# First stage of a hybrid encoder block: instructions in written order, five of eight row blocks of the conditioning matrix through TensorE, x loads behind the matrix

## The chip, the cores and the metric

The kernel runs on one core of one Trainium2 chip. The metric is the device time of one execution in microseconds (us). Before the change it is 1370.64 us, the median of 3 runs (1370.08 to 1372.82).

## The reference

One layer of a bidirectional encoder for 2048 tokens of width 1024, all in float32. What matters here is its beginning: a conditioning vector `c` makes three vectors of 1024 through a 1024 x 3072 matrix; two of them scale and shift the normalised tokens, which are then projected.

```python
mod = silu(c) @ w_ada + b_ada
shift, scale, gate = split(mod, 3)
h = rmsnorm(x, norm_w) * (1 + scale) + shift
proj = h @ w_in + b_in          # 9 groups of 512 columns and 16 gate columns
# neighbourhood attention on four groups, a two-way mLSTM on five and the gates
y = concat(na_out, ml_out) @ w_out
out = rmsnorm(x + gate * y, final_norm_w)
```

## The kernel before, in words

Tokens lie in four groups g of 512 (`GT`), each of four tiles `tt` of 128; the model width lies in eight blocks k of 128 (`KT`). h is kept transposed, width on the partitions, as a rounded part `hhi[g]` and the remainder `hlo[g]`; weights are split alike into `whi` and `wlo`. So each product is three matmuls (hi hi, hi lo, lo hi; L452 to L456 and L507). Weight blocks of 256 columns alternate between two slots: a (block 0 with the 16 gate columns, so 272) and b (block 1), then blocks 2, 3 and so on.

`start` (L209 to L400) is the first stage; `tok_blocks` (L582) follows and begins with block 2. In `start`:

- **x.** `load_x` (L222) loads a tile of x, 512 KB. `prep_x` (L228) squares it on ACT, takes reciprocal roots (`rsqrt`, 12 small steps: on POOL for the first group, else on DVE) and scales x (ACT for the first group, L239, else DVE, L241). x tiles of groups 0, 1 and 3 share four buffers, those of group 2 have a pool of their own.
- **The conditioning matrix.** Shift is part 0 and scale part 1, each in two quarters q of 512 columns. `ada_tile(part, q, kt)` (L243) loads one row block of a quarter, 128 x 512 (256 KB, seven buffers `wada`), and DVE multiplies it by its entry of silu(c) per partition and adds it to `acc`: eight row blocks a quarter, four quarters, 32 products (L249, L251). `columns` (L253) sums `acc` over the partitions with four 1-column matmuls against `ones` into the one PSUM buffer `sp`, which leaves the quarter as columns; ACT copies it and POOL adds the bias `bada`, and for the scale adds 1 and multiplies by `norm_w` (L260 to L266). The results are `shT` and `gT`.
- **h of group 0.** `turned(k)` (L270) transposes four x tiles on PE into PSUM `tp` (three buffers). `first_h(k)` (L275, k 0 to 3) makes hhi and h on ACT, hlo on POOL. For k 4 to 7 the scale is applied first (`scaled`, L283) and the shift later (`shifted`, L287), since the shift's second quarter comes last.
- **Projection.** `vo_first(g)` (L498) multiplies a whole group with slot a, k outermost, into four PSUM banks (`pp` has four): 12 matmuls per k. `vo_group` (L510) takes the sums out on DVE (L524, L526), and for slot b multiplies tile by tile, 24 matmuls each. The loop at L375 does this for every group. After each tile it steps a chain (`next_h`, L359) that prepares the next group's h (`make_h`, L293: transposes, hhi on ACT, h on DVE, hlo on POOL).
- **Stores and fills.** The output tile of a `vo_group` is stored by SP at the next flush; `table_fills` (L555) writes constants to nine tables in DRAM.

The program is written with a scheduler that orders the instructions of each engine by itself: before the change the order in `start` is the scheduler's, led by the order of the text. Nearly all loads are issued by SP, in order. An instruction that waits holds up those behind it on its engine or queue.

Of the kernel before, what the change touches and what calls it, by code (L numbers as in the profile page):

```python
# [8 lines left out]
F32 = mybir.dt.float32  # L9
F32R = mybir.dt.float32r  # L10
AF = mybir.ActivationFunctionType
ALU = mybir.AluOpType
# [3 lines left out]
P = 128  # L16
D = 1024
T = 2048
KT = D // P
NG = 4  # L20
GT = 512
# [8 lines left out]
BIG = 1e30  # L30
# [32 lines left out]
class Kernel:  # L63
# [64 lines left out]
    def small_loads(self):  # L128
        nc = self.nc
        nc.sync.dma_start(self.bcol, self.b_col)  # L130
        nc.sync.dma_start(self.cw, self.conv_w)
        nc.sync.dma_start(self.cb, self.conv_b)
        nc.sync.dma_start(self.mlw, self.ml_w)
        nc.vector.tensor_scalar(self.bcol[:, 0:4], self.bcol[:, 0:4], -0.125, None, ALU.mult)


    def phase1(self):
# [4 lines left out]
        self.hhi = [ht012.tile([P, KT, GT], F32R, name=f"hhi{g}") for g in range(3)]  # L142
        self.hlo = [ht012.tile([P, KT, GT], F32R, name=f"hlo{g}") for g in range(3)]
# [36 lines left out]

        self.phase1b(left, right)


    def stage_tile(self, name):
        self.stages.reverse()
# [23 lines left out]
    def start(self, left):  # L209
# [5 lines left out]
        nc.sync.dma_start(cact, self.cT)  # L215
        nc.scalar.activation(cact, cact, AF.Silu)
# [3 lines left out]
        xt = {}  # L220

        def load_x(tt):  # L222
            pool = early if tt // 4 == 2 else xp
            t = pool.tile([P, D], F32, tag="x", bufs=4, name=f"x_{tt}")
            nc.sync.dma_start(t, self.x[tt * P : (tt + 1) * P, :])
            xt[tt] = t

        def prep_x(tts):  # L228
            n = len(tts)
            ssq = xp.tile([P, n], F32, tag=f"ssq{n}", bufs=2, name=f"ssq_{tts[0]}")  # L230
            rst = xp.tile([P, n], F32, tag=f"rst{n}", bufs=2, name=f"rst_{tts[0]}")
            for i, tt in enumerate(tts):
                junk = xp.tile([P, D], mybir.dt.bfloat16, tag="junk", bufs=1, name=f"junk_{tt}")
                nc.scalar.activation(junk, xt[tt], AF.Square, accum_out=ssq[:, i : i + 1])
            nc.vector.tensor_scalar(ssq, ssq, 1.0 / D, EPS, ALU.mult, ALU.add)
            self.rsqrt(xp, rst, ssq, f"x{tts[0]}", nc.gpsimd if tts[0] == 0 else None)
            for i, tt in enumerate(tts):
                if tt < 4:
                    nc.scalar.activation(xt[tt], xt[tt], AF.Copy, scale=rst[:, i : i + 1])  # L239
                else:  # L240
                    nc.vector.tensor_scalar(xt[tt], xt[tt], rst[:, i : i + 1], None, ALU.mult)  # L241

        def ada_tile(part, q, kt):  # L243
            w = ada.tile([P, GT], F32, tag="wada", bufs=7, name=f"wada_{part}_{q}_{kt}")
            c0 = part * D + q * GT
            nc.sync.dma_start(w, self.w_ada[kt * P : (kt + 1) * P, c0 : c0 + GT])
            a = acc[:, c0 : c0 + GT]
            if kt == 0:
                nc.vector.tensor_scalar(a, w, cact[:, kt : kt + 1], None, ALU.mult)  # L249
            else:  # L250
                nc.vector.scalar_tensor_tensor(a, w, cact[:, kt : kt + 1], a, ALU.mult, ALU.add)  # L251

        def columns(part, q):  # L253
            ps = self.sp.tile([P, 4], F32, tag="sp", name=f"mod_{part}_{q}")
            j0 = part * 8 + 4 * q
            for j in range(4):
                nc.tensor.matmul(ps[:, j : j + 1], acc[:, (j0 + j) * P : (j0 + j + 1) * P], self.ones[:, 0:1], start=True, stop=True)
            dst = (self.shT, self.gT)[part][:, 4 * q : 4 * q + 4]
            if part or q == 0:
                nc.scalar.activation(dst, ps, AF.Copy)  # L260
                nc.gpsimd.tensor_tensor(dst, dst, bada[:, j0 : j0 + 4], ALU.add)
            else:
                nc.vector.tensor_add(dst, ps, bada[:, j0 : j0 + 4])
            if part:
                nc.gpsimd.tensor_scalar(dst, dst, 1.0, None, ALU.add)
                nc.gpsimd.tensor_tensor(dst, dst, nw[:, 4 * q : 4 * q + 4], ALU.mult)  # L266

        tps = {}

        def turned(k):  # L270
            tps[k] = self.tp.tile([P, GT], F32, tag="tp", name=f"tp_0_{k}")
# [30 lines left out]
            nc.vector.tensor_scalar(h, tp, self.gT[:, k : k + 1], self.shT[:, k : k + 1], ALU.mult, ALU.add)  # L302
            nc.gpsimd.tensor_tensor(lo, h, hi.bitcast(F32), ALU.subtract)

        for tt in range(4):
            load_x(tt)
        prep_x([0, 1, 2, 3])
        for kt in range(KT):
            ada_tile(1, 0, kt)
            if kt == 2:  # L310
                nc.sync.dma_start(bada, self.b_ada)
                nc.sync.dma_start(nw, self.norm_w)
        self.load_w(0, 0, (0,))
        rg = xp.tile([P, KT, 16], F32, name="rg")
        hi, lo = self.wslot[0]
        nc.sync.dma_start(rg, self.w_gate)
        nc.scalar.activation(hi[:, :, 256:], rg, AF.Copy)
        nc.gpsimd.tensor_tensor(lo[:, :, 256:], rg, hi[:, :, 256:].bitcast(F32), ALU.subtract)
        for kt in range(KT):
            ada_tile(0, 0, kt)  # L320
        columns(1, 0)
        for k in range(3):
            turned(k)
        columns(0, 0)
        for kt in range(KT):
            ada_tile(1, 1, kt)
        self.load_w(0, 0, (1,))
        self.chain = iter(())
        first = self.vo_first(0)
        for k in range(4):  # L330
            first_h(k)
            if k == 0:
                turned(3)
        for k in range(4):
            if k:
                turned(k + 3)
            if k == 2:
                columns(1, 1)
            next(first)
        for kt in range(KT):  # L340
            ada_tile(0, 1, kt)
            if kt >= 4:
                scaled(kt)
                if kt == 4:
                    turned(7)
        columns(0, 1)
# [7 lines left out]
        early_s = ExitStack()  # L354
        early = self.pool(early_s, "early", bufs=1)
        self.load_w(1, 1)
        self.small_loads()

        def next_h(tiles):  # L359
            for _ in range(2):  # L360
                yield
            prep_x(tiles)
            yield
            for k in range(0, KT, 2):
                make_h(tiles, k)
                make_h(tiles, k + 1)
                yield

        fills = self.table_fills()

        def fill(g):
            for _ in range(3 if g >= 2 else 0):
                next(fills, None)

        for g in range(NG):  # L375
            nxt = [4 * g + 4 + j for j in range(4)] if g < NG - 1 else []
            for tt in nxt:
                load_x(tt)
            if nxt:
                self.chain = next_h(nxt)  # L380
            if 0 < g < 3:
                for _ in self.vo_first(g):
                    pass
            self.vo_group(0, 0, g, g < 3)
            fill(g)
            if not nxt:
                self.load_w(2, 0)
                self.load_bias(2)
            self.vo_group(1, 1, g)
            fill(g)  # L390
            if g == 1:
                for _ in self.chain:
                    pass
                early_s.close()
                ht3 = self.pool(left, "ht3", bufs=1)
                self.hhi.append(ht3.tile([P, KT, GT], F32R, name="hhi3"))
                self.hlo.append(ht3.tile([P, KT, GT], F32R, name="hlo3"))
        for _ in fills:
            pass
        self.flush()  # L400
# [153 lines left out]

    def table_fills(self):  # L555
        nc = self.nc
        nc.gpsimd.memset(self.big, BIG)
# [1152 lines left out]
```

## Time and profile before

| | |
|---|---|
| median of 3 runs | 1370.64 us |
| profiled execution | 1360.06 us |
| its span | 1358.3 us |
| PE busy | 1284.1 us (95%), 8204 matmuls |
| DVE busy | 796.4 us (59%) |
| ACT busy | 517.8 us (38%) |
| POOL busy | 288.7 us (21%) |
| mean granted TensorE clock | 0.995 |
| DMA | 263.29 MB, mean 194 GB/s |

PE is TensorE's matmuls, PEld its weight loads, DVE VectorE, ACT ScalarE, POOL GpSimd, SP the engine that issues most DMAs. A row of a view in order of time reads: start, duration, engine, line of the kernel, operation, output<-inputs, shapes, count, and in brackets the idle time before it and what ended it. A matmul of two float32 operands is recorded as two instructions, so four 1-column matmuls of `columns` stand as x8; a transpose stands as one.

### The profile page before, as it was taken

The page shows a single profiled execution, that of the slowest core. Times are in us where ns is not written, and L with a number is a line of the kernel's source. Part 1 is how long each engine was busy: PE and PEld are TensorE (multiplying, and loading weights), DVE is VectorE, ACT ScalarE, POOL GpSimd, SP SyncE. Part 2 cuts the span into 40 slices and gives each one's busy share as a digit, 9 for nine tenths or more (in the row PEclk, how much of TensorE's full clock was granted, in tenths as well). Part 3 has the DMA queues.
Part 4 walks back from the last instruction along what each step waited for, and adds up shares of the span by engine and source line. Part 5 has one row for each costly group of instructions (what it writes and reads, how often), then busy time and mean ns, then how long its engine had stood idle before and what let it go on. Part 6 is the DMA issues. An engine that isn't in the chain of part 4 may idle for free.

```text
span 1358.3 us, 23412 instructions
## 1 busy us (share of the span) xinstructions
PE 1284.1 (95%) x8204; PEld 1099.9 (81%) x8204; DVE 796.4 (59%) x2436; ACT 517.8 (38%) x1113; POOL 288.7 (21%) x322
## 2 busy tenths in 40 slices
PE   2989899999899999999989999999999999999996
PEld 2989899999788787888878878778877777778785
DVE  6683623111274569156867868867737676666664
ACT  4642213344432323113313323313346565555552
POOL 4454301335301110001212102212202211212121
PEclk9999999999999999999999999999999999999998
DMA  9799533599877675564676777667688986768871
GB/s 330 219 287 238 190 101 103 138 227 229 217 161 193 137 188 158 174 172 140 202 203 190 235 233 204 215 182 203 177 265 244 217 216 179 185 176 194 201 184 47
DMA packets 244425, 263.29 MB, mean 194 GB/s; under 512 B 31943, under 2 KB 200135, under 8 KB 244307
## 3 DMA queue, kind: packets, MB, share of 16 engines
q1 hardware_dynamic: 161374, 190.38, 51.0%
q0 software_dynamic: 20496, 36.21, 11.1%
q10 hardware_dynamic: 62436, 35.20, 9.2%
q8 instruction: 65, 1.06, 0.3%
q14 instruction: 54, 0.43, 0.1%
HBM read 177.18 MB, written 92.72 MB: 199 GB/s over the span
## 4 chain that ended last, share of the span: by engine, by line
PE 39%; DMA 10%; DVE 7%; issue 6%; POOL 1%; SPq 1%; ACT 1%; ACTq 0%; POOLq 0%; DVEq 0%
PE pq L892 16%; PE y L1459 10%; DMA tab<-d_t 4%; DMA kv<-d_ck 3%; PE pT L1399 3%; PE pO L1414 2%; PE pS L1371 2%; DVE acc_q L834 2%; PE pi L1120 2%; PE px L1118 2%; PE dc L1066 1%; DMA hlo<-d_wo 1%; SPq L576 1%; PE a L1105 1%; DMA d_ck<-acc_k 1%
## 5 line engine op out<-in xcount | busy, mean ns | idle before, releaser
L892 PE MATMUL pq<-hhi,whi_a 128*128 128x512 f32 x512 | 207.7, 406 | 0.8 <-ACT u L797 0.8
L892 PE MATMUL pq<-hlo,whi_a 128*128 128x512 f32 x512 | 208.1, 406 | 0.0
L892 PE MATMUL pq<-hhi,wlo_a 128*128 128x512 f32 x512 | 207.3, 405 | 0.0
L892 PEld LDWEIGHTS pq<-hhi,whi_a 128*128 128x128 f32 x512 | 96.8, 189 | 18.0 <-ACT u L797 1.2
L892 PEld LDWEIGHTS pq<-hlo,whi_a 128*128 128x128 f32 x512 | 96.7, 189 | 16.6 <-issue 0.5
L892 PEld LDWEIGHTS pq<-hhi,wlo_a 128*128 128x128 f32 x512 | 96.8, 189 | 16.5
L1401 ACT ACTIVATE pt<-pT 96x384 f32<-96x384 f32 (+3 forms) x128 | 65.8, 514 | 84.5 <-PE pT L1399 81.6
L1380 ACT ACTIVATE pbuf<-pbuf,mn 128x480 f32<-128x480 f32 (+5 forms) x128 | 76.1, 596 | 52.3 <-DVE mn L1379 52.2
L1459 PE MATMUL y<-hhi,whi_a 128*128 128x512 f32 x256 | 90.6, 415 | 0.5 <-ACT whi_a L1429 0.5
L1459 PE MATMUL y<-hhi,wlo_a 128*128 128x512 f32 (+1 forms) x272 | 90.6, 399 | 0.2 <-ACT y L1466 0.2
L1379 DVE CUSTOM_DVE_ANT_0 pbuf<-pS,tab 128x480 f32<-128x480 f32 (+5 forms) x128 | 63.0, 539 | 38.4 <-PE pS L1371 29.3
L1142 POOL TENSOR_TENSOR hm<-hm,ck 128x128 f32<-128x128 f32 x64 | 26.3, 412 | 268.4 <-DVE hm L1141 228.2
L866 POOL TENSOR_TENSOR wlo_a<-rawq,whi_a 128x1024 fp32r<-128x1024 f32 x20 | 48.3, 2413 | 153.3 <-ACT whi_a L865 115.3
L1123 ACT ACTIVATE num<-px,gtile 128x129 f32<-128x129 f32 x120 | 38.3, 364 | 109.5 <-PE px L1118 92.3
L1050 DVE TENSOR_SCALAR wv<-kv,gtile 128x129 f32<-128x129 f32 x120 | 37.8, 323 | 65.7 <-DMA kv<-d_ck 33.1
L524 DVE TENSOR_TENSOR stvo<-pvo,brow 128x256 f32<-128x256 f32 x64 | 26.4, 420 | 82.0 <-PE pvo L456 63.4
L454 PE MATMUL pvo<-whi_b,hhi 128*128 128x256 f32 x256 | 74.2, 290 | 0.2 <-DVE gates L526 0.2
L1399 PE MATMUL pT<-ident,pbuf 128*128 128x128 f32 (+2 forms) x416 | 66.9, 274 | 7.7 <-DVE pbuf L1391 6.3
L1399 PEld LDWEIGHTS pT<-ident,pbuf 128*128 128x128 f32 (+2 forms) x416 | 50.4, 136 | 29.3 <-issue 8.9
L455 PE MATMUL pvo<-wlo_b,hhi 128*128 128x256 f32 x256 | 72.8, 284 | 0.0
L456 PE MATMUL pvo<-whi_b,hlo 128*128 128x256 f32 x256 | 72.8, 284 | 0.0
L739 ACT ACTIVATE dec<-dec,gtile 128x128 f32<-128x128 f32 x128 | 42.2, 392 | 57.2 <-POOL dec L732 44.3
(296 smaller groups left out, 3418.6 us busy)
## 6 DMA issues: line engine op xcount, KB each, us to landing
ck<-d_ck SPq DMA_DIRECT2D x64, 384.5 KB
kv<-d_ck SPq DMA_DIRECT2D x120, 128.5 KB
rawq<-in_w_main_dram SPq DMA_DIRECT2D x28, 512.0 KB
raw<-in_w_main_dram SPq DMA_DIRECT2D x20, 512.0 KB
d_ck<-stvo SPq DMA_DIRECT2D x16, 514.0 KB
x<-in_x_dram SPq DMA_DIRECT2D x16, 512.0 KB
wada<-in_w_ada_dram SPq DMA_DIRECT2D x32, 256.0 KB
dec<-d_mneg SPq DMA_DIRECT2D x32, 256.0 KB
```

The lines of the kernel that those rows point to most:

```text
L454: nc.tensor.matmul(ps, lhi(k), rhi(k), start=(k == 0), stop=False)
L455: nc.tensor.matmul(ps, lhi(k), rlo(k), start=False, stop=False)
L456: self.mark = nc.tensor.matmul(ps, llo(k), rhi(k), start=False, stop=(k == KT - 1))
L739: nc.scalar.activation(t[:, o, :], t[:, o, :], AF.Exp, bias=self.cols["g"][:, d, h, c : c + 1])
L866: nc.gpsimd.tensor_tensor(lo[:, :, cs], raw, hi[:, :, cs].bitcast(F32), ALU.subtract)
L892: self.mark = nc.tensor.matmul(patch_ps(ps) if patch else ps, w, self.htok(h, g, k, patch), start=(k == 0 and n == 0), stop=(k == KT - 1 a ...
L1123: nc.scalar.activation(num[:, d, :], px[:, d, :], AF.Copy, scale=self.cols["inter"][:, d, h, c : c + 1])
L1379: nc.vector.tensor_tensor_reduce(pt[:, :nk], ps, tabs[place[u]][j][:, :nk], 1.0, 3e38, ALU.add, ALU.min, mn)
L1380: nc.scalar.activation(pt[:, :nk], pt[:, :nk], AF.Exp, bias=mn, scale=-1.0, accum_out=sums[:, j : j + 1])
L1399: nc.tensor.transpose(ps[:cs, i, :], U[u][j][:, i * cs : (i + 1) * cs], self.ident)
L1401: nc.scalar.activation(t[:cs, :nch, :], ps[:cs, :nch, :], AF.Copy)
L1459: nc.tensor.matmul(y, m[:, k, :], w[k][:, cs], start=(k == 4 and n == 0), stop=(k == 3 and n == 2))
```

## The change

- `start` runs inside `manual_schedule`: each engine does its instructions in the order of the text, which is written out anew.
- Of the eight row blocks of a quarter, DVE still adds kt 0, 2 and 4 (`summed`). kt 1, 3, 5, 6 and 7 go to PE (`added`): the block itself is the stationary operand, in four pieces of 128 columns, and the column of silu(c) the moving one, so that the sums arrive in PSUM as columns at once. DVE's three blocks join as a sixth `added` against `ones` (`total`), and the bias first of all, by a product with the identity. A quarter holds the one `sp` buffer from that product until `columns` reads it.
- `columns` is one operation: DVE for the scale ((sum + 1) x norm_w), ACT for the shift.
- Roots are on DVE for every group. `bada` and `nw` are loaded from ACT's queue.
- The x tiles of groups 1 and 2 are loaded into the room of hhi of a later group, so they need no free x buffer. They and group 3's are issued behind the last row block of the matrix.
- Transposes of the next group spread: k 0 to 3 beside slot b, k 4 after it, k 5 to 7 between the steps of `vo_first`, which group 3 uses too. Squares stand beside k 4 to 7.
- The `big` memset moves to the front, a scaling of `bcol` (`scale_bias`) behind group 1, a part of block 1's split from POOL to DVE, and the fills are spread anew. Block 2's weights are loaded and split beside group 3's slot b.

The core of the diff:

```diff
-        self.start(left)
+        with self.tc.manual_schedule():
+            self.start(left)
...
+        def summed(part, q, kt, w):
+            c0 = part * D + q * GT
             a = acc[:, c0 : c0 + GT]
             if kt == 0:
                 nc.vector.tensor_scalar(a, w, cact[:, kt : kt + 1], None, ALU.mult)
             else:
                 nc.vector.scalar_tensor_tensor(a, w, cact[:, kt : kt + 1], a, ALU.mult, ALU.add)
+        def added(ps, left, right, last):
+            for j in range(4):
+                nc.tensor.matmul(ps[:, j : j + 1], left[:, j * P : (j + 1) * P], right, start=False, stop=last and j == 3)
+
+        def quarter(part, q):
+            ws, parts = {}, iter([False] * 5 + [True])
+            ps = mods[part, q] = self.sp.tile([P, 4], F32, tag="sp", name=f"mod_{part}_{q}")
+            j0 = part * 8 + 4 * q
+            nc.tensor.matmul(ps, self.ident, bada[:, j0 : j0 + 4], start=True, stop=False)
+            def load(kt):
+                ws[kt] = ada_tile(part, q, kt)
+            def step(kt):
+                if kt in (0, 2, 4):
+                    summed(part, q, kt, ws.pop(kt))
+                else:
+                    added(ps, ws.pop(kt), cact[:, kt : kt + 1], next(parts))
+            def total():
+                c0 = part * D + q * GT
+                added(ps, acc[:, c0 : c0 + GT], self.ones[:, 0:1], next(parts))
+            return load, step, total
...
+        for tt in four:
+            load_x(tt)
+        load, step, total = quarter(1, 0)
+        for kt in range(KT):
+            load(kt)
...
+        for tt in four:
+            square(tt, ssq)
+        step(0)
+        rst = roots(four, ssq)
+        for kt in range(1, KT):
+            step(kt)
+        total()
+        columns(1, 0)
+        part = self.raw_w(0, 0, (0,))[0]
...
+        load, step, total = quarter(0, 0)
+        for kt in range(KT):
+            load(kt)
+        for tt in four:
+            scale_x(tt, rst)
+        part()
...
         for kt in range(KT):
+            step(kt)
+            if kt == 4:
+                for k in range(3):
+                    turned(k)
+                total()
         columns(0, 0)
+        load, step, total = quarter(1, 1)
...
+        first_h(0)
+        step(0)
+        step(1)
+        first_h(1)
+        next(first)
+        turned(3)
+        step(2)
+        step(3)
+        first_h(2)
+        next(first)
+        turned(4)
+        step(4)
+        step(5)
+        first_h(3)
+        next(first)
+        turned(5)
+        total()
+        step(6)
+        step(7)
+        part()
+        next(first)
+        turned(6)
+        columns(1, 1)
+        load, step, total = quarter(0, 1)
         for kt in range(KT):
+            load(kt)
+        step(0)
+        parts = self.raw_w(1, 1)
...
+        for tt in range(4, 8):
+            load_x(tt)
+        for k in range(4, KT):
+            step(k - 3)
+            scaled(k)
+            if k == 4:
+                turned(7)
+        step(5)
+        total()
+        step(6)
+        step(7)
+        columns(0, 1)
         for k in range(4, KT):
             shifted(k)
             next(first)
+        parts[0]()
+        parts[1](nc.vector)
...
+            self.vo_group(0, 0, g, True)
+            if tiles:
+                rst = roots(tiles, ssq)
+                for tt in tiles:
+                    scale_x(tt, rst)
```

More of the change, by code (lines that the diff above doesn't have):

```diff
@@ L141, in phase1 @@
         ht012 = self.pool(left, "ht012", bufs=1)
-        self.hhi = [ht012.tile([P, KT, GT], F32R, name=f"hhi{g}") for g in range(3)]
-        self.hlo = [ht012.tile([P, KT, GT], F32R, name=f"hlo{g}") for g in range(3)]
+        self.hpools = {g: ht012 for g in range(3)}
+        self.hhi, self.hlo = [], []
+        for g in range(2):
+            self.token_tiles(g)
         self.gcols = self.pool(right, "gcols", bufs=1, side="right")
@@ L181, in phase1, with token_tiles @@
         self.phase1b(left, right)
+    def token_tiles(self, g):
+        for part, held in (("hi", self.hhi), ("lo", self.hlo)):
+            held.append(self.hpools[g].tile([P, KT, GT], F32R, tag=f"h{part}{g}", name=f"h{part}{g}"))
     def stage_tile(self, name):
@@ L251, in ada_tile @@
                 nc.vector.scalar_tensor_tensor(a, w, cact[:, kt : kt + 1], a, ALU.mult, ALU.add)
-        def columns(part, q):
[L254 to L261, printed above, removed]
-            else:
[L263 to L268, printed above, removed]
+        def added(ps, left, right, last):
[11 more added lines that the diff above has]
+                    summed(part, q, kt, ws.pop(kt))
+                else:
+                    added(ps, ws.pop(kt), cact[:, kt : kt + 1], next(parts))
[3 more added lines that the diff above has]
+            return load, step, total
+        def columns(part, q):
+            qs = slice(4 * q, 4 * q + 4)
+            ps = mods.pop((part, q))
+            if part:
+                nc.vector.scalar_tensor_tensor(self.gT[:, qs], ps, 1.0, nw[:, qs], ALU.add, ALU.mult)
+            else:
+                nc.scalar.activation(self.shT[:, qs], ps, AF.Copy)
+        tps, mods = {}, {}
         def turned(k):
@@ L367, in next_h, with next_w @@
                 yield
+        def next_w():
+            for part in self.raw_w(2, 0):
+                yield
+                part()
         fills = self.table_fills()
-        def fill(g):
-            for _ in range(3 if g >= 2 else 0):
-                next(fills, None)
[L375 to L397, printed above, removed]
+        self.chain = iter(())
```

126 lines of the change are left out of this document (69 added, 57 removed).

## The prediction

> **What bounds the kernel now.** I read the page first, then the busy time of each engine by stage, then PE's instructions in order of time, then what the first of them waited for.
>
> ```profile
> span 1358.3 us, 23412 instructions
> ```
> ```profile
> 0.00:34.00 34.00, 9.05 (x36) 7.28 (x37) 21.36 (x30) 14.90 (x23) 14.44 (x29) 1.00 0.93 330
> 34.00:68.00 34.00, 32.03 (x238) 31.14 (x239) 20.52 (x44) 22.27 (x36) 14.22 (x11) 0.95 0.70 219
> 238.00:272.00 34.00, 34.00 (x290) 34.00 (x289) 5.69 (x15) 12.23 (x29) 12.37 (x8) 1.00 0.56 141
> ```
>
> The second fence is the table by stage; its columns are PE, PEld, DVE, ACT and POOL busy, granted clock, DMA share and GB/s. From 238 to 272 PE is busy for all 34 us: the kernel runs at PE's pace once it has started, and PE is nearly idle only in the first 34 us (9.05). So I take a delay or gain of PE in the first stage as a delay or gain of the end, one for one. PE's marks in that stage:
>
> ```profile
> 19.03 4.02 PE L273 MATMUL tp<-ident,x 128*128 128x128 f32 x12 [19.03 <-ACT x L239]
> 22.84 1.71 PE L257 MATMUL mod<-ones,acc 128*128 128x1 f32 x8
> 24.81 1.86 PE L257 MATMUL mod<-ones,acc 128*128 128x1 f32 x8 [0.26 <-ACT gT L260]
> 31.77 0.59 PE L507 MATMUL pvo<-whi_a,hhi 128*128 128x272 f32 x1 [5.09 <-ACT hhi L280]
> 45.85 0.39 PE L507 MATMUL pvo<-whi_a,hhi 128*128 128x272 f32 x1 [1.59 <-ACT hhi L290]
> 53.73 0.28 PE L454 MATMUL pvo<-whi_b,hhi 128*128 128x256 f32 x1
> 156.06 0.36 PE L454 MATMUL pvo<-whi_a,hhi 128*128 128x256 f32 x1 [1.30 <-DVE stvo L524]
> ```
>
> The first projection matmul starts at 31.77, the first group's slot-0 work ends at 53.73, and block 2, the first of the next stage, begins at 156.06. I forecast these three marks. What holds the first one:
>
> ```profile
> 9.19 1.06 ACT L234 ACTIVATE junk<-x 128x1024 bf16<-128x1024 f32 x1
> 10.83 0.63 POOL L1230 TENSOR_TENSOR nwt_x<-rst 128x4 f32<-128x4 f32 x1 [9.25 <-DVE rst L1217]
> 17.37 0.42 POOL L1233 TENSOR_TENSOR rst<-rst,nwt_x 128x4 f32<-128x4 f32 x1
> 27.10 2.33 POOL L203 TENSOR_TENSOR wlo_a<-raw,whi_a 128x1024 fp32r<-128x1024 f32 x1
> 30.26 0.65 POOL L261 TENSOR_TENSOR shT<-shT,bada 128x4 f32<-128x4 f32 x1
> 32.47 6.36 POOL L281 TENSOR_TENSOR hlo<-h,hhi 128x512 fp32r<-128x512 f32 x4 [1.56 <-ACT h L280]
> 30.94 0.78 ACT L280 ACTIVATE hhi<-tp,shT,gT 128x512 fp32r<-128x512 f32 x1 [4.05 <-POOL shT L261]
> 9.89 0.49 DVE L249 TENSOR_SCALAR acc<-wada,cact 128x512 f32<-128x512 f32 x1 [8.87 <-DMA wada<-in_w_ada_dram]
> 10.65 5.47 DVE L251 SCALAR_TENSOR_TENSOR acc<-wada,cact,acc 128x512 f32<-128x512 f32 x7
> 32.88 8.86 DVE L251 SCALAR_TENSOR_TENSOR acc<-wada,cact,acc 128x512 f32<-128x512 f32 x7 [0.24 <-DMA wada<-in_w_ada_dram]
> ```
>
> The squares end at 10.3 (9.19 + 1.06). The reciprocal roots then take POOL 7 us (10.83 to 17.8). Two POOL jobs then stand before the shift's bias (27.10 to 30.26), and only then can ACT make the first h (30.94). DVE multiplies the matrix's row blocks at 5.47/7 = 0.78 us each, and the last quarter ends at 32.88 + 8.86 = 41.7, which PE feels as the 1.59 us at 45.85.
>
> **The change part by part.** *Roots to DVE.* The same roots of a later group show the price on DVE:
>
> ```profile
> 60.03 0.17 DVE L235 TENSOR_SCALAR ssq<-ssq 128x4 f32<-128x4 f32 x1
> 62.62 0.16 DVE L1233 TENSOR_TENSOR rst<-rst,nwt_x 128x4 f32<-128x4 f32 x1
> ```
>
> That is 2.8 us, so x is scaled from about 13.3 on, not 17.8. The gain is hidden if PE is late, and below it is. Biases folded into PSUM and into one DVE operation take POOL off the path (about 4 us). The two loads on ACT's queue (bada, nw) stand before the squares, in ACT's wait for x until 5.22 us; I cost them at nothing, and 0.9 us if that wait were gone.
>
> *Row blocks on PE.* A quarter now has six sums on PE (five blocks and a total), each of four 1-column products, and one identity product. Each sum is exactly one `mod` group of before, x8 in the rows. So 24 groups stand where 4 stood. Their price hangs on the clock:
>
> ```profile
> 38.51 0.95 PE L257 MATMUL mod<-ones,acc 128*128 128x1 f32 x8
> 39.32 0.38 PE L507 MATMUL pvo<-whi_a,hhi 128*128 128x272 f32 x1
> 32.16 0.43 PE L507 MATMUL pvo<-wlo_a,hhi 128*128 128x272 f32 x1
> 32.39 0.43 PE L507 MATMUL pvo<-whi_a,hhi 128*128 128x272 f32 x1
> 32.62 1.05 PE L273 MATMUL tp<-ident,x 128*128 128x128 f32 x4
> 103.69 0.29 PE L507 MATMUL pvo<-whi_a,hhi 128*128 128x272 f32 x1
> 115.63 0.29 PE L507 MATMUL pvo<-whi_a,hlo 128*128 128x272 f32 x1
> 116.55 0.36 PE L454 MATMUL pvo<-whi_b,hhi 128*128 128x256 f32 x1
> 119.48 1.04 PE L298 MATMUL tp<-ident,x 128*128 128x128 f32 x8
> 120.27 0.36 PE L454 MATMUL pvo<-whi_b,hhi 128*128 128x256 f32 x1
> ```
>
> Slow against fast: a sum takes 1.71 (22.84) or 39.32 - 38.51 = 0.81; twelve 272-column matmuls take 12 x 0.23 = 2.73 or 12 x (115.63 - 103.69)/95 = 1.51; four transposes take 1.05 or (120.27 - 119.48)/2 = 0.40. Which price holds? The granted clock in windows of 3.41 us:
>
> ```profile
> 22.59:26.01 3.42, 3.16 (x17) 3.07 (x15) 3.22 (x6) 1.32 (x3) 1.09 (x2) 1.00 0.97 337
> 43.07:46.49 3.42, 1.83 (x16) 1.66 (x14) 0.82 (x2) 3.42 (x7) 2.35 (x1) 1.00 0.00 0
> 46.49:49.90 3.41, 3.40 (x16) 3.26 (x15) 2.08 (x4) 2.08 (x3) 1.25 (x1) 0.50 0.68 180
> 780.35:783.77 3.42, 1.68 (x9) 0.99 (x7) 0.00 (x0) 1.38 (x4) 0.00 (x0) 1.00 1.03 334
> ```
>
> The clock column shows only what was granted again after a loss, so the slow start stands at 1.00. Two readings decide. In 22.59 to 26.01 PE is busy for 3.16 us, nearly all with 1-column products, and the products after it (24.81 + 1.86 = 26.67) are as slow as before. In 43.07 to 46.49 it is busy for 1.83 us, of which 0.95 are such products, and the clock falls to 0.50 in the next window; yet 1.68 us of 512-column matmuls at 780 cost nothing. I conclude that 1-column products do not count as work that earns the clock, and price sums slow wherever PE does little else.
>
> The Trainium skill, TensorE: Matmul & The Clock Gate, Part 1, speaks against this: about 3.4 us of sustained matmul activity release the full clock. By that rule PE, fed from 10.7 us on, would run its sums fast from about 16 on; that is rival B. Its Part 4 says that transposes do not count as PE-busy in the same way; no row here has transposes alone.
>
> *The schedule of PE, slow sums.* Row blocks land no faster than they do now, kt 1 by 10.65.
> - Quarter (1,0): 10.65 + 6 x 1.71 = 20.9. The next identity product waits for the one `sp` buffer until DVE has read it, 0.35 by the 0.26 wait at 24.81: 21.3.
> - Quarter (0,0): 0.43 + 6 x 1.71 + three transposes 3.15: 35.1. The shift is copied: 35.5.
> - ACT makes hhi 0 (0.78) and h (the same) by 37.0, POOL hlo 0 (6.36/4 = 1.59) by 38.5. PE does the identity and one sum of (1,1) meanwhile, so the first projection matmul starts at **37.6 against 31.77**; the third waits for hlo 0. k 0 ends at 40.8.
> - k 1 with a transpose and a sum: slow 5.49, fast 2.72. k 2 the same. k 3 with three sums and two transposes: slow 9.96, fast 4.74. Quarter (0,1) with one transpose: slow 11.74, fast 5.46. Columns and the shift of k 4: 1.2. k 4 to 7, 48 matmuls: 4.5 us slow, then fast, 8.0; all fast 6.0. (One window is 3.4 and two are 6.8; after the wait at 45.85 it was over at 49.90.)
> - My choice: k 1 slow (46.3), k 2 and k 3 fast since half of PE's time there is wide matmuls (53.8), one window of (0,1) fast and the last 2.6 sums slow (61.7), then 1.2 and 8.0: **70.9 against 53.73**. All slow is 82.7; all fast after k 0 is 63.6.
>
> DVE falls from eight products a quarter to three; what it gives up hides behind PE. What PE waits on is not the matrix's DMA: at the 330 GB/s of the first stage's row, the 2.1 MB of a quarter land in 6.4 us, against 10.3 of sums. The written order itself I cost at nothing outside this list: each engine's waits in it are the ones named here; what they may cost besides is bounded with the rest below, 0 to 9.7. Behind a sum that waits for its block stand the transposes and wide matmuls of the next k, which is why the list is added up in order.
>
> *Loads moved.* On SP the last block of (0,1) waits for DVE's first product of that quarter (about 54), and behind it stand block 1's weights, the biases and x 4 to 7. The splits on ACT and POOL and the squares on ACT wait for those: 3.1 MB at 330 GB/s are there by about 63.5, and ACT turns to the splits at 63 and to the squares at 65. That is hidden; with fast sums (rival B) the same loads would land at 50 for an ACT that is ready at 48, which costs up to 2 us. x 8 to 15 come a group early.
>
> *After 53.73.* Before takes 102.3 us to block 2. Its matmuls alone are three groups of 96 at 0.1257 (36.2), sixteen runs of 24 at 119.48 - 116.55 = 2.93 (46.9), and 24 transposed blocks at 0.40 (9.5): 92.6. The other 9.7 are waits and slow clock:
>
> ```profile
> PE tp L298 <- DVE h L302: 3.7, 3, 2.2
> 90.20 0.66 PE L298 MATMUL tp<-ident,x 128*128 128x128 f32 x4 [2.20 <-DVE h L302]
> 82.51 1.06 ACT L234 ACTIVATE junk<-x 128x1024 bf16<-128x1024 f32 x1 [7.88 <-DMA x<-in_x_dram]
> ```
>
> Late x (82.51) makes the late h that PE waits for at 90.20. With x there early, squares beside k 4 to 7 and transposes spread over k, I let 3 us remain, between 0 and 9.7 (nearer 0, since the largest has its cause removed; the 1.3 at 156 stays): 95.6, a gain of 6.7.
>
> *The sum.* 70.9 + 95.6 = 166.5 against 156.06: +10.4. On the profiled execution's 1360.06 (span 1358.3 and 1.8 around it) that is 1370.5; the median shown is 1370.64, 10.6 above that execution, so I add the difference to it: **1381.0**. The other cases use the same rest.
>
> **The rivals.**
> - B, the sums earn the clock. Three sums slow, then fast: (1,0) ends at 18.2, (0,0) with its copy at 25.2, k 0 at 29.5 (hlo 0 from POOL at 28.2), k 3 at 39.7, (0,1) at 45.1, slot 0 at 52.3. With the rest 147.9: -8.1, **1362.5, faster**. For it: nearly unbroken feeding from 10.7 on, six times longer than the sample at 22.59. Against: that window and the fall at 46.49. It decides from the point where 1-column products release the clock.
> - C, wide matmuls keep the clock through (0,1): 63.6, +3.1, **1373.8**. For it: 1.68 us of wide work were enough at 780. Against: (0,1) has none.
> - D, never fast before k 4: 82.7, +22.2, **1392.9**. For it: k 1 and 2 are only half wide matmuls, and less than that lost the clock at 43.07.
>
> **How the numbers follow.** A 0.50, B 0.24, C 0.13, D 0.13. A's own range, with 0 to 9.7 in the rest and the window's phase, is 1375 to 1388. The whole reaches to B and leaves out D: 1360 to 1389. Within 0.2% (2.7 us, about what a measurement tells apart) lies half of C: 0.07; faster 0.24, slower 0.69.
>
> **What would show it.** Right: the products at 11 to 35 us all near 1.7 per eight; DVE idle beside them; the first projection matmul near 37.6; PE free of waits for h after slot 0; block 2 near 166. Wrong: products falling to 0.8 per eight by 18 us (B), a clock of 1.00 through (0,1) (C), or a shift at block 2 that is not found at the end.

## The result and the profile after

| | before | after |
|---|---|---|
| median | 1368.18 us (18 runs, 1363.69 to 1372.82) | 1376.16 us (18 runs, 1371.45 to 1383.81) |
| ratio | | 1.0063, 95% interval 1.0047 to 1.0079 |
| profiled execution | 1360.06 us, span 1358.3 | 1382.7 us, span 1380.9 |
| second profile, see the experiments | 1367.42 us, span 1365.6 | 1369.45 us, span 1367.7 |

The kernel after is slower by 0.6%. The first profiled execution of before is below all its timed runs, and that of after near the top of its own; so 22.6 us between those two profiles overstate it, and a second profile of each stands beside them below. PE's marks, read in its order of time as in the prediction (us):

| | first projection matmul | slot 0 done | block 2 begins | conv stage begins | it ends | span |
|---|---|---|---|---|---|---|
| forecast | 37.6 | 70.9 | 166.5 | | | |
| after | 37.33 | 74.94 | 170.97 | 360.5 | 559.1 | 1380.9 |
| after, second profile | 36.77 | 68.48 | 162.15 | 350.1 | 543.8 | 1367.7 |
| before | 31.77 | 53.73 | 156.06 | 348.2 | 538.6 | 1358.3 |
| before, second profile | 31.40 | 53.99 | 153.14 | 347.1 | 540.1 | 1365.6 |

The conv stage, which follows the token stage that block 2 opens, is told from the others by its first `pc` and `pq` matmuls. The table of the kernel after by stage (PE, PEld, DVE, ACT and POOL busy, granted clock, DMA share, GB/s):

```profile
0.00:34.00 34.00, 23.30 (x109) 23.19 (x109) 7.67 (x25) 11.50 (x16) 3.69 (x9) 1.00 0.71 242
34.00:68.00 34.00, 32.72 (x176) 32.07 (x175) 3.78 (x7) 11.22 (x18) 7.44 (x5) 0.79 0.61 201
68.00:102.00 34.00, 34.00 (x271) 34.00 (x272) 19.93 (x47) 20.07 (x31) 12.73 (x13) 0.96 0.99 258
```

PE is busy for 23.30 us of the first 34 instead of 9.05, DVE for 3.78 us of the second 34 instead of 20.52. Work went from DVE, which had time, to PE, which sets the end. In the second stretch PE is busy as long as before (32.72 against 32.03), but with 176 matmuls in place of 238, at a clock of 0.79. PE in order of time:

```profile
11.01 8.67 PE L273 MATMUL mod<-cact,wada 128*128 128x1 f32 x40 [1.31 <-DMA wada<-in_w_ada_dram]
19.53 1.85 PE L273 MATMUL mod<-ones,acc 128*128 128x1 f32 x8
...
25.49 2.80 PE L309 MATMUL tp<-ident,x 128*128 128x128 f32 x12
28.09 1.71 PE L273 MATMUL mod<-ones,acc 128*128 128x1 f32 x8
29.65 5.26 PE L273 MATMUL mod<-cact,wada 128*128 128x1 f32 x24
...
37.33 0.57 PE L602 MATMUL pvo<-whi_a,hhi 128*128 128x272 f32 x1
...
41.29 1.71 PE L273 MATMUL mod<-cact,wada 128*128 128x1 f32 x8
...
46.57 0.99 PE L273 MATMUL mod<-cact,wada 128*128 128x1 f32 x8
...
62.49 3.55 PE L273 MATMUL mod<-cact,wada 128*128 128x1 f32 x16
67.06 0.59 PE L602 MATMUL pvo<-whi_a,hhi 128*128 128x272 f32 x1 [1.01 <-ACT hhi L326]
...
158.01 0.35 PE L549 MATMUL pvo<-whi_b,hhi 128*128 128x256 f32 x1 [2.05 <-DVE gates L621]
```

Read the counts: x40 is five sums of eight, in 8.67 us, 1.71 each and a small tail. From 11 to 20 PE does nothing but such products, without a gap, and they never get shorter; nor do they from 28 to 35. Between wide matmuls, at 46.57, one takes 0.99. Behind slot 0 PE waits only once more before block 2, 2.05 us at 158. Now the clock around the last sums, in windows of 3.41 us (in the kernel before, half clock lasts one such window, from 46.49 to 49.90; here it lasts 17.07 us, from 53.39 to 70.46, which is five windows):

```profile
49.98:53.39 3.41, 3.41 (x31) 3.41 (x30) 1.13 (x3) 0.97 (x2) 0.00 (x0) 1.00 0.27 72
53.39:56.80 3.41, 3.41 (x19) 3.41 (x18) 0.93 (x2) 0.98 (x2) 0.00 (x0) 0.51 0.76 233
...
67.04:70.46 3.42, 3.40 (x13) 3.12 (x14) 2.73 (x4) 3.42 (x5) 0.59 (x1) 0.50 0.05 20
70.46:73.87 3.41, 3.41 (x29) 3.41 (x28) 2.60 (x1) 3.35 (x6) 1.91 (x3) 0.99 0.81 256
```

PE is full in the window before the fall, 3.41 of 3.41 us, but its first 2.07 us are sums (to 52.05) and only 1.34 wide matmuls; the clock goes at 53.39. From 54.91 to 66.0 there are sums with four transposes between them; up to 63.63 PE is just as busy in each window, and the clock stays away. It is back at 70.46, behind the first full window of wide matmuls (from 67.06).

### The profile page after: what moved, and what is told of

Same layout as the page of the kernel before. It is cut to its first block, busy times and chain, and to the rows that moved or that the text cites. A ratio compares the mean times of both kernels' runs of the same rounds, so it can differ in the third digit from the quotient of the medians.

```text
span 1380.9 us, 23691 instructions
## 1 busy us (share of the span) xinstructions
PE 1325.0 (96%) x8372; PEld 1142.5 (83%) x8372; DVE 769.9 (56%) x2430; ACT 518.6 (38%) x1112; POOL 272.7 (20%) x302
## 4 chain that ended last, share of the span: by engine, by line
PE 41%; DMA 11%; issue 6%; DVE 5%; POOL 1%; ACT 1%; SPq 0%; ACTq 0%; DVEq 0%; POOLq 0%
PE pq L986 17%; PE y L1553 8%; DMA tab<-d_t 6%; DMA kv<-d_ck 3%; PE pT L1493 2%; PE pO L1508 2%; PE pc L551 2%; PE pc L550 2%; PE pc L549 2%; PE pi L1214 2%; PE pS L1465 2%; PE px L1212 2%; PE dc L1160 1%; DVE pbuf L1473 1%; DMA hlo<-d_wo 1%
## 5 line engine op out<-in xcount | busy, mean ns | idle before, releaser
L1474 ACT ACTIVATE pbuf<-pbuf,mn 128x480 f32<-128x480 f32 (+5 forms) x128 | 76.1, 595 | 53.8 <-DVE mn L1473 53.8
```

Source lines behind the costliest of these rows:

```text
L1474: nc.scalar.activation(pt[:, :nk], pt[:, :nk], AF.Exp, bias=mn, scale=-1.0, accum_out=sums[:, j : j + 1])
```

## The experiments

The first four ran on one chip, where before's median was 1363.37 us; the next four on another (1364.74), the last three on a third (1362.87). Ratios are to before on the same chip.

**All row blocks on VectorE.** Order, roots and early x loads stay as after; no row block goes through TensorE.

```diff
-            ws, parts = {}, iter([False] * 5 + [True])
+            ws, parts = {}, iter([True])
-                if kt in (0, 2, 4):
+                if True:
```

(`total` moves behind the last step of each quarter.)

> The changed kernel with all eight row blocks of every quarter on DVE again (PE only sums DVE's result, one group of eight 1-column products a quarter); the written order, the roots on DVE and the early x stay. If the sums on PE at half clock are the whole loss: DVE is done with quarter (1,0) at 18.7, PE's sum at 20.6, (0,0) at 26.7 and 28.5, the first projection matmul at 29.7 (37.33 in the changed kernel, 31.77 before); slot 0 of the first group ends near 55 (74.94 and 53.73), block 2 begins near 149.5 (156.06 before), so about 0.995 of the time before. Rival, the written order is the loss and the products only stand in it: the first projection matmul stays near 37, slot 0 near 75, and the time stays at 1.006.

1355.4 us, ratio 0.9941 (0.9919 to 0.9963): faster than both. First matmul at 30.41, slot 0 done at 58.62, block 2 at 151.96. The direction is as expected, slot 0 and block 2 are 2 to 4 us late. The profile says why:

```profile
27.46 1.87 PE L273 MATMUL mod<-ones,acc 128*128 128x1 f32 x8 [2.78 <-DVE acc L269]
...
47.72 1.87 PE L273 MATMUL mod<-ones,acc 128*128 128x1 f32 x8 [3.48 <-DVE acc L269]
```

Now PE waits for DVE's products, 2.78 and 3.48 us. So DVE did need relief in this order, but the price paid for it was higher. What remains of the change without the sums is a gain of 0.6%. Only the sums were undone here, so it is they that turn this gain into a loss.

**Wide matmuls between the sums.** To the kernel after: thirty 512-column bf16 matmuls of no use ahead of the first sum, and two behind each sum of (1,0) and (0,0). They go to a PSUM tile that nobody reads.

```diff
+        def wide(n):
+            for _ in range(n):
+                nc.tensor.matmul(wps, warm[:, 0:P], warm, start=True, stop=True)
+        wide(30)
...
                 nc.tensor.matmul(ps[:, j : j + 1], ...)
+            if held[0]:
+                wide(held[0])
```

> The changed kernel with the clock held in its first two quarters: 30 wide matmuls (128x512, bf16, into an unused PSUM bank, read by nobody) before the first sum, and two more after each sum of quarters (1,0) and (0,0). Half clock as the price: sums fall from 1.71 to 0.81 plus 0.43 for the two wide ones, (1,0) ends near 18.5, (0,0) near 27.8, the first projection matmul at 29 and slot 0 near 62 instead of 74.94, although PE is given more work. Rival, the sums are slow for another cause (their blocks have just landed, or a weight load of 128 float32 columns costs that): they stay at 1.7 and the extra work makes the first projection matmul later, near 42.

1378.39 us, ratio 1.0104 (1.0069 to 1.0138); first matmul at 36.68, slot 0 done at 69.42. In order of time:

```profile
10.90 1.03 PE L273 MATMUL mod<-cact,wada 128*128 128x1 f32 x8
11.80 0.59 PE L313 MATMUL wps<-warm 128*128 128x512 bf16 x2
...
15.32 1.71 PE L273 MATMUL mod<-cact,wada 128*128 128x1 f32 x8
16.89 1.01 PE L313 MATMUL wps<-warm 128*128 128x512 bf16 x2
...
27.61 2.77 PE L321 MATMUL tp<-ident,x 128*128 128x128 f32 x12
30.17 1.39 PE L273 MATMUL mod<-ones,acc 128*128 128x1 f32 x8
31.43 0.59 PE L313 MATMUL wps<-warm 128*128 128x512 bf16 x2
31.86 0.95 PE L273 MATMUL mod<-cact,wada 128*128 128x1 f32 x8
32.67 0.59 PE L313 MATMUL wps<-warm 128*128 128x512 bf16 x2
33.10 0.95 PE L273 MATMUL mod<-cact,wada 128*128 128x1 f32 x8
```

The clock was there at 10.90 and gone by 15.32: the granted clock falls at 14.0, behind a window with 1.28 us of the fillers in it (10.61 to 14.02). At half clock two wide ones per sum, 0.80 of every 2.37 us (17.69 - 15.32 in that view), a third of the time, did not bring it back. It is back at 31.1, behind the twelve transposes, and through the window that follows (31.09 to 34.50, 1.56 us of fillers) the same two per sum do hold it: the sums at 31.86 and 33.10 take 0.95. Neither number that I had expected came: for most of the first two quarters the fillers failed. That they cost time is not shown: the first matmul comes no later than in the kernel after (37.33, and 36.77 in its second profile, below), and the interval overlaps with that of the kernel after.

**Wide matmuls ahead only.** The thirty without the twos.

> The changed kernel with only the 30 wide matmuls before the first sum, none between the sums. If 1-column products neither earn nor hold the clock: between one and two windows of 3.4 us after the last wide matmul run at full clock, so four to eight sums at 0.81, then 1.71 again; the first projection matmul between 32.5 and 35. Rival, they hold a clock that was once granted: all twelve sums at 0.81, the first projection matmul near 26.

One run, 1369.04 us; the first matmul, at 32.85, lies where the theory had it, but only in part for its reason.

```profile
10.52 1.03 PE L273 MATMUL mod<-cact,wada 128*128 128x1 f32 x8
11.75 1.05 PE L273 MATMUL mod<-cact,wada 128*128 128x1 f32 x8 [0.19 <-DMA wada<-in_w_ada_dram]
13.10 5.18 PE L273 MATMUL mod<-cact,wada 128*128 128x1 f32 x24 [0.30 <-DMA wada<-in_w_ada_dram]
...
24.11 2.80 PE L318 MATMUL tp<-ident,x 128*128 128x128 f32 x12
26.70 1.05 PE L273 MATMUL mod<-ones,acc 128*128 128x1 f32 x8
27.61 2.82 PE L273 MATMUL mod<-cact,wada 128*128 128x1 f32 x24
```

The same instruction, eight products, is short at 10.52 and 11.75 and long from 13.10 on: given the full clock, the products lose it within 3 us. It comes back behind the twelve transposes (26.70), and x24 takes 2.82 where it took 5.18. Two sums were short behind the wide matmuls, not four to eight; the other four short ones stand behind the transposes, which the theory did not count on. So 1-column products neither earn the clock nor hold it. Rival B needed them to earn it; it is out.

**One half of the sums each.** First the two lead-in quarters (1,0) and (0,0) on VectorE and the two in slot 0, (1,1) and (0,1), as after; then the reverse, with `pe` the other way round.

```diff
-                if kt in (0, 2, 4):
+                if kt not in pe:      # pe = () for q == 0, else (1, 3, 5, 6, 7)
```

> The changed kernel with quarters (1,0) and (0,0) all on DVE, (1,1) and (0,1) still five of eight on PE. If the two halves of the loss add up: first projection matmul at 29.7 as with all on DVE, then the 37.6 us to the end of slot 0 that the changed kernel takes, so 67.3, and block 2 at 161.8: a time between the changed kernel and all on DVE, about 1.003 of before. Rival, the loss is all in the first two quarters: slot 0 ends near 55.

> Quarters (1,0) and (0,0) as in the kernel after (five of eight row blocks through TensorE), quarters (1,1) and (0,1) with all eight row blocks on VectorE. Theory (one-column products neither earn nor hold the granted clock, so eight of them take 1.71 us instead of 0.81): the lead-in is untouched, first projection matmul at 37.3 us; without the sums in slot 0 this slot takes what it took with everything on VectorE, 28.2 us, so it ends at 65.5 and block 2 starts at 159; time 1.003 of before, give or take 0.004. Rival (the sums inside slot 0 are innocent and the lost clock is a matter of where the windows fall): slot 0 takes 37.6 us again, ends at 75, block 2 at 168 to 170, time 1.007 or more.

The first (lead-in on VectorE): 1372.31 us, ratio 1.0059 (1.0033 to 1.0085), slot 0 done at 62.93, block 2 at 156.40. The second: 1367.87 us, ratio 1.0014 (0.9990 to 1.0038), first matmul at 35.44, slot 0 at 63.45, block 2 at 156.56. Both theories gave their marks 2 to 5 us too late (67.3 and 161.8, 65.5 and 159), and both rivals are further off (55; 75 and 168). The time of 1.003 that both forecast held for the second and lies just below the interval of the first. Slot 0 itself lasts 32.1 us with sums in it and 28.0 without, against 28.2 with none anywhere. With the kernel after and the one with none this makes a square of marks at block 2:

| | sums of slot 0 on DVE | on PE |
|---|---|---|
| lead-in on DVE | 151.96 | 156.40 |
| lead-in on PE | 156.56 | 162.15 and 170.97 |

Each half costs some 4.5 us by itself. Three of these four marks are of one execution each, and two executions of the kernel after lie 8.8 us apart; the marks nearer by bear it out. The first projection matmul comes at 30.41 and 30.84 with the lead-in on VectorE and at 35.44, 36.77 and 37.33 with it on PE, and slot 0 lasts 28.0 and 28.2 us without sums and 32.1, 31.7 and 37.6 with them (the last two are the kernel after). The times are less tidy (0.9941, 1.0059, 1.0014, 1.0063): the first kernel's 1372.31 is more than its mark explains (its profiled execution took 1367.36, so what is missing lies partly in other executions), and where that came from stays open.

**The start written out anew, all on VectorE.** DVE does the next quarter's first products before it reads the last quarter's columns, and the transposes stand earlier.

```diff
         for kt in range(KT):
             step(kt)
-            if kt == 4:
-                for k in range(3):
-                    turned(k)
-                total()
+            if kt == 2:
+                columns(1, 0)
+                for k in range(3):
+                    turned(k)
+        total()
         columns(0, 0)
...
+        for kt in range(KT):
+            step(kt)
         first_h(0)
-        step(0)
-        step(1)
         first_h(1)
```

> All row blocks on VectorE and the start written out anew, so that VectorE adds the next quarter's products before it evacuates the columns of the last, and TensorE turns x tiles earlier. Theory (written order pays, the TensorE sums are the loss, and VectorE was what slot 0 waited for in the kernel with all row blocks on VectorE): first projection matmul at 27.6 us, slot 0 22 us long and done at about 50, block 2 at 143 to 145, time 0.985 to 0.990 of before. Rival (slot 0 is bound by matrix and weight arrivals, not by VectorE): first matmul at 27.6 to 30, slot 0 still 28 us, block 2 at 149 to 152, time 0.991 to 0.994, the same as with all row blocks on VectorE.

1353.09 us (1352.8 to 1354.85), ratio 0.9910 (0.9890 to 0.9930): the lowest here, though its interval overlaps with that of all row blocks on VectorE in the first order (0.9919 to 0.9963). Marks 29.87, 55.76 and 149.39: the theory's 50 and 143 to 145 were missed, and the rival's marks came nearly as it gave them (slot 0 lasts 25.9 us, not 28). Slot 0 is not bound by DVE alone. Around its second half, in the columns of the table by stage:

```profile
42.40:45.80 3.40, 1.82 (x15) 1.66 (x14) 2.26 (x3) 1.71 (x3) 0.00 (x0) 1.00 0.65 200
45.80:49.20 3.40, 2.38 (x10) 2.06 (x10) 2.36 (x4) 3.29 (x6) 0.00 (x0) 0.50 0.87 331
49.20:52.60 3.40, 3.40 (x17) 3.40 (x17) 2.41 (x2) 3.37 (x6) 2.50 (x3) 0.50 1.03 412
```

PE had 1.82 us of work in one stretch while it waited for the last quarter, and runs at half clock in the next two.

**Both kernels again,** unchanged.

> The kernel after, unchanged, a second profile and five more rounds. Theory (the shift at block 2 and the longer conv stage are the kernel's own): first projection matmul at 37.3 us, block 2 at 166 to 171, conv stage 195 to 199 us; time 1.004 to 1.008 of before. Rival (the 198.6 us of its conv stage was that one execution): conv stage 190 to 192 us, and the difference to before is then carried by the mark at block 2 alone.

> The kernel before, unchanged, a second profile and five more rounds. Theory (conv stage is shorter in this kernel's order of instructions than in the order that the scheduler gives all kernels with the written start): conv stage 190 to 191.5 us, block 2 at 156, time 0.999 to 1.001 of before. Rival (the conv stage varies from execution to execution, whatever the order): conv stage anywhere from 190 to 199 us.

After: 1376.49 us, ratio 1.0080 (1.0049 to 1.0111). Before: 1365.48 us, ratio 0.9998 (0.9983 to 1.0012). The marks stand in the first table; the conv stage, 198.6 and 190.4 us in the first profiles, is 193.7 and 193.0 here. So both theories missed on the conv stage (195 to 199, 190 to 191.5), and on block 2 (162.15 against 166 to 171, 153.14 against 156); for the kernel before it is the rival, a stage that varies, that came. The second profile of after at the end of slot 0:

```profile
40.59 0.95 PE L273 MATMUL mod<-cact,wada 128*128 128x1 f32 x8
...
55.86 3.55 PE L273 MATMUL mod<-cact,wada 128*128 128x1 f32 x16
60.43 0.59 PE L602 MATMUL pvo<-whi_a,hhi 128*128 128x272 f32 x1 [1.02 <-ACT hhi L326]
```

The sum that took 1.71 us at 41.29 in the first profile takes 0.95 at 40.59 here: the clock came back 6 us earlier (by 40.59, not by 46.57), the sums of (0,1) were done 6.6 us earlier (the first wide matmul behind them at 60.43, not 67.06), and three windows were at half clock instead of five. Same kernel, same order: slot 0 lasts 31.7 us and not 37.6. Counted back in windows of 3.41 us, from 54.03 where the clock goes here and from 53.39 in the first profile, the wide matmuls of k 0 fill 3.12 us of the window that ends at 40.38 here, and 2.41 us of the one that ends at 39.74 there, where it did not come back. So 5.9 us hang on where the windows fall.

**x late again.** In the kernel after, the loads of x 4 to 15 go back to the head of each group's loop.

```diff
-        for tt in range(4, 8):
-            load_x(tt)
...
             tiles = [tt + 4 for tt in now] if g < NG - 1 else []
+            for tt in tiles:
+                load_x(tt)
```

> The kernel after with one part undone: the x tiles 4 to 15 are loaded at the head of each group's loop, as before, in place of behind the matrix. Theory (the early x loads took away nothing that the written order hadn't taken away already; what costs is the sums): slot 0 ends at 68 to 75 us, from there to block 2 93 to 96 us as in the kernel after, time 1.005 to 1.010 of before. Rival (the early x loads are what shortened this stretch from 99 to 102 us to 94 to 96): the stretch is back at 99 us or more, block 2 at 168 or later, time 1.011 or more.

1374.72 us, ratio 1.0072 (1.0048 to 1.0095); slot 0 done at 68.97, from there to block 2 94.0 us. As the theory had it: the early loads bring nothing that can be measured in this order.

**Without the written order.** The kernel after with the scheduler ordering the first stage.

```diff
-        with self.tc.manual_schedule():
-            self.start(left)
+        self.start(left)
```

> The kernel after without the written order: the same sums through TensorE and the same early x loads, but the scheduler orders the first stage. Theory (the written order is worth some 5 us at block 2, as all row blocks on VectorE in written order showed, and the sums cost 10): block 2 at 168 us or later, time 1.010 or more of before. Rival (the written order itself brings nothing, the early loads do, and a scheduler finds better places for the sums): block 2 at 155 to 165, time 1.006 or less.

1384.55 us, ratio 1.0151 (1.0115 to 1.0188): slot 0 done at 70.63, block 2 at 175.55, 104.9 us from the one to the other against 93.7 to 96.0. Block 2 and time are as the theory had them. PE's waits in that stretch:

```profile
PE pvo L548 <- DVE gates L620: 5.3, 2, 3.1
PE pvo L601 <- POOL stvo L607: 1.3, 1, 1.3
PE pvo L601 <- POOL hlo L338: 1.2, 2, 0.7
PE tp L333 <- DVE xs L254: 0.4, 1, 0.4
```

Columns: total us, times, longest. They come to 8.2 us, against the one wait of 2.05 (or 1.2, in the second profile) in the written order. So the written order is what shortened this stretch; which part of it did was not tried.

**Wide matmuls in the gap.** To the best kernel: six ahead of the last quarter's sums and four behind, where PE waited.

```diff
+        wide(6)
         total()
+        wide(4)
         columns(0, 1)
```

> The kernel with all row blocks on VectorE in the newly written start (ratio 0.991), with six 512-column bf16 matmuls of no use ahead of the last quarter's sums and four behind them, where TensorE waited 1.58 and 1.02 us. Theory (a window of 3.41 us with too few wide matmuls loses the clock for the next two): the granted clock stays at 1.0 from 42 to 56 us where it was 0.50 for 6.8 us, slot 0 ends at 53 to 54 instead of 55.8, block 2 at 146.5 to 147.5 instead of 149.4, time 0.987 to 0.990 of before. Rival (ten wide matmuls are too few, as two per sum were): clock 0.50 again, slot 0 at 56 or later, time 0.991 to 0.993.

1354.3 us, ratio 0.9936 (0.9912 to 0.9961). Marks 30.30, 55.09 and 148.34.

```profile
42.40:45.80 3.40, 3.35 (x26) 2.80 (x26) 2.34 (x4) 1.95 (x3) 0.00 (x0) 1.00 0.61 188
45.80:49.20 3.40, 3.00 (x19) 2.02 (x18) 1.03 (x2) 1.96 (x4) 0.00 (x0) 1.00 0.75 258
49.20:52.60 3.40, 3.40 (x28) 3.40 (x28) 2.40 (x4) 3.40 (x5) 1.59 (x1) 1.00 0.94 383
```

The clock held, as the theory had it, and the 48 matmuls behind the gap took 6.9 us instead of 8.9 (55.09 - 48.19, 55.76 - 46.85). But they began 1.3 us later: at k 1 the clock had come back 3 us later in this execution (the 272-column matmuls get short at 38.59, and at 35.40 without fillers). So slot 0 (55.09), block 2 (148.34) and the time all missed the theory (53 to 54, 146.5 to 147.5, 0.987 to 0.990). The time shows no gain over the kernel without fillers (0.9936 against 0.9910, on different chips), so as a recipe it stays unproven.

## Why the prediction was right, and where it was not

- **Sums at half clock** (1.71 each): held. (1,0) ended at 21.4 and, in the second profile, at 20.8 (forecast 20.9), (0,0) at 34.9 and 34.4 (35.1), the first projection matmul came at 37.33 and 36.77 (37.6). The Trainium skill, TensorE: Matmul & The Clock Gate, Part 1, says that about 3.4 us of sustained matmul activity release the clock; the trace doesn't agree where that activity is 1-column float32 products: 10.4 us of them released nothing. A reading of mine was wrong: I wrote that no row before has transposes alone, but the twelve at 19.03 are alone on PE for 4.02 us, and the sum behind them (22.84) is still slow.
- **k 1 slow, k 2 and k 3 at full clock**: held in the first profile. In the second the clock was back at k 1 already.
- **(0,1): one window at full clock, then slow, slot 0 done at 70.9**: that sums lose the clock held, when they lose it did not, and the size is a spread. In the first profile k 3 was done at 53.77 (forecast 53.8), but the clock went at 53.39, ahead of (0,1), and slot 0 ended at 74.94; in the second it went some 3 us into (0,1), and slot 0 ended at 68.48. k 4 to 7 took 7.9 and 8.1 us (8.0). Rivals C (clock kept through (0,1)) and D (no full clock before k 4) did not occur.
- **95.6 us from slot 0 to block 2**: 96.0 and 93.7. The reason I gave was half wrong. I put the gain to early x; with x late it was 94.0 still. The written order did it; that it was its spread transposes is not shown, and of the 8.2 us of waits without it 5.3 are for `gates`.
- **Written order at nothing outside the list**: its gain was left out. It is worth some 10 us in the rest (104.9 without). The rest came out as forecast because I had put down a gain there to early x; that is luck. The sums then cost more than that gain: +14.6 at block 2 (the mean of 170.97 and 162.15 less 151.96).
- **Block 2 at 166.5, +10.4**: the two profiles' mean is 166.6, against 154.6 of before's two: +12.0. That the middle was hit so closely is luck; the two lie 8.8 apart.
- **A delay at block 2 is one at the end, one for one**: true of the sum only. From block 2 to the end of the conv stage nothing was edited, yet the token stage became shorter (189.5 and 188.0 us against 192.1 and 194.0) and the conv stage longer (198.6 and 193.7 against 190.4 and 193.0). Means: -4.3 and +4.5; they cancel. The scheduler orders these stages anew. The conv stage, in the columns of the table by stage, in both profiles of before and then of after:

```profile
348.00:539.00 191.00, 186.85 (x834) 150.63 (x835) 118.97 (x231) 63.15 (x104) 24.25 (x12) 1.00 0.70 175
347.00:540.20 193.20, 189.48 (x833) 152.72 (x834) 120.29 (x234) 63.31 (x104) 24.07 (x12) 0.98 0.68 174
360.50:559.20 198.70, 191.52 (x833) 153.93 (x834) 121.43 (x231) 63.56 (x102) 26.99 (x12) 0.97 0.68 171
350.00:544.00 194.00, 187.40 (x835) 150.13 (x835) 120.57 (x229) 63.42 (x102) 26.16 (x12) 1.00 0.67 176
```

PE is idle for 4.2 and 3.7 us of it before and for 7.2 and 6.6 us after: some 3 us come with the kernel. The rest is PE at a lower granted clock (0.97 and 0.98), which one execution of each kernel shows and the other does not.

All kernels here with the written start have one order of instructions in the conv stage on PE, DVE and ACT, and it is not that of before; their conv stage took 193.4 to 198.6 us, their token stage 186.9 to 189.5. PE's waits in the conv stage, in the kernel before:

```profile
PE pc L454 <- DVE stv L489: 3.1, 1, 3.1
PE kt L845 <- ACT acc_k L835: 2.5, 3, 1.6
```

and in the kernel after:

```profile
PE kt L939 <- ACT acc_k L929: 6.1, 4, 2.0
PE pc L549 <- DVE stv L584: 2.7, 1, 2.7
```

The wait for `acc_k` more than doubles (5.5 against 2.8 in the second profiles). That this order is its cause was not tried by itself; the kernel without the written order, with yet another order on PE there, took 197.5 us for the conv stage and 186.7 for the token stage.

- **The end**: 1381.0 was forecast, 1376.16 measured, inside the range of my choice (1375 to 1388). Of these 4.8 us, 2.4 are the shift (+8.0 in the runs of the result, +11.8 where both kernels ran again, 10.4 forecast) and 2.5 the base: 1370.64 was the median of three runs, 1368.18 that of eighteen.

## What to carry to other kernels

Work that goes from an idle engine to the one that sets the end must be priced at the clock that this work itself leaves there: here, of 24 groups of 1-column products, 0.81 us each at full clock, 20 ran at half clock at about 1.71 in the first profile and 16 in the second, and matmuls behind them were slow too. An instruction order and a change of engines that come in one edit are to be timed apart; here one gains and the other loses. Take two profiles before a shift of a few us is explained from one.

## What the runs showed of the hardware that I had not expected

- Transposes can earn the clock, and what decides it stays open. Behind twelve of them (2.80 us) it was full in two kernels: at 26.70 in the one with wide matmuls ahead, and within the sum at 30.17 in the one with wide matmuls between. It was not in the kernel after, where the same twelve (25.49 to 28.29) lie across a window's border: counted back in windows of 3.41 us from 53.39, one falls at 26.08. In the fullest window they are busy for 2.80 and 2.71 us in the two kernels that got the clock, for 2.21 in the kernel after, but also for 2.62 in the kernel with late x (24.27 to 27.68) and, in four bursts, for 2.99 in the kernel before (19.18 to 22.59), and neither of these got it. So the share of one window does not settle it. The Trainium skill, TensorE: Matmul & The Clock Gate, Part 4, says that transposes do not count as PE-busy in the same way; the first two kernels speak against it, the others do not.
- A PE that is busy all the time can lose the clock: what held it here was the share of wide matmuls in a window. Lost behind windows of 3.41 us with 1.34 us of them (49.98 to 53.39 in the kernel after) and 1.28 (10.61 to 14.02 with wide matmuls between); held behind 1.56 (31.09 to 34.50 there) and 1.76 (46.56 to 49.98 in the kernel after, beside sums and four transposes). So a share of some 1.4 to 1.5 of 3.41 us divides these windows. In the gap of the last kernel ten bf16 ones beside other wide work held it.
